# Between the two layers of a diffusion backbone: modulation weights partly into spare expert buffers, a gate store issued by ScalarE, the square-root table fetched early, half of the normalised rows scaled on ScalarE

## The chip, the cores and the metric

One core of a Trainium2 chip runs the whole program. The metric is the device time of one execution in microseconds (us), the median of several runs. The engines are TensorE (PE in the profile; its weight loads are PEld), VectorE (DVE), ScalarE (ACT), GpSimd (POOL) and SyncE (SP, which here only issues transfers). Sixteen DMA engines move the data.

## The reference

Two layers over 1024 latent tokens and 256 context tokens of width 1024, all in 32-bit floats. In each layer:

```python
mod_l = (s_lat @ ada_w[layer] + ada_b[layer])        # six rows: shift, scale, gate, twice
h_l = _rmsnorm(x, norm_mix_g[layer]) * (1.0 + sc_a) + sh_a
p_l = h_l @ w_in[layer]
...
x = x + g_a * (concat(three mixers of p_l, p_c) @ w_out[layer])
h = _rmsnorm(x, norm_ffn_g[layer]) * (1.0 + sc_f) + sh_f
x = x + g_f * _ec_ffn(h, router_w, exp_w1, exp_w3, exp_w2)     # 16 experts
```

The modulation rows depend on the conditioning alone, not on `x`. Layer 1 reads the `x` that the last expert of layer 0 has added to.

## The kernel before

A layer runs in stages: projection, three mixers, output projection, routing, 16 experts. Two places matter here: the start of a projection, in either layer, and the seam where layer 0's experts end and layer 1's projection begins (1880 us to 1920 us of the span).

**Experts** (`moe`). Expert weights arrive by SP's queue in 1 MB tiles `ew`, in a ring of 6 buffers (pool `raws`). ScalarE rounds each to `ewH` and VectorE takes the rest as `ewL`, and TensorE multiplies. Gathered tokens lie in `xg0`, their transpose in `xT0`, its two halves of precision in `xH` and `xL`, all in the pool `wk`, two buffers each, for expert e and e+1. The last product of an expert is added to `x` in memory (the tensor `xd`, and `xc` for the context) by an accumulating scatter that GpSimd issues (L1961).

**Modulation** (`ada_steps`). A third of a layer's modulation, called block b, is a product of a 1024 by 2048 slice of `ada_w` with the conditioning: 8 loads, 32 matmuls per half of them (L159, `adaw`), a bias (L298, tile `mod`), four transposes, a copy (L309, `modT`) and small copies into the tables `modS` and `modA`. Layer 1's blocks 0 and 1 are computed in layer 0's `moe`: block 0 during routing, block 1 after the last expert. With `raws` given, each of its 8 loads is 1 MB into a buffer of the expert ring (L269). Block 1 also holds a gate, which two transfers store to memory (L304).

**Projection** (`project`, `norm_T`). For each 128 tokens: a load `xt` (L362), a sum of squares on ScalarE (L381) for even tiles and on VectorE (L378) for odd ones, for each two tiles a root on ScalarE (L384) and a reciprocal on VectorE (L385), the scaled row `xn` on VectorE (L388), transposes on TensorE (L393), then scale and shift by the modulation on ScalarE (L400, `h`), rounding (L401) and the rest (L402). `first` does the four tiles of block 0 before any product can start; block 1 (four tiles) and the context block (two) are interleaved with the products of the block before. A projection weight arrives as `raw` (L476, two buffers), ScalarE rounds it (L169, `wH`), GpSimd takes the rest (L170, `wL`).

**What sets the order.** A scheduler orders the instructions of each engine when the program is built; routing and the first expert's fetch keep their written order. Each engine, and each engine's queue of transfers, runs its list strictly in that order: a transfer that waits holds all transfers behind it in the same queue.

Of the kernel before, what the change touches and what calls it, by code (L numbers as in the profile page):

```python
# [138 lines left out]
class Net:  # L139
# [115 lines left out]

    def ada_steps(self, l, b, wp, nk, raws=None):

# [4 lines left out]
        w = I["ada_w"][l]  # L262
        st = {}

        def load(i):
            wt = []
            if raws:
                t = raws.tile([128, 4, 512], F32, name="adaw", tag="ew")
                nc.sync.dma_start(t.rearrange("p g c -> p (g c)"), w[i * 128:(i + 1) * 128, 2048 * b:2048 * b + 2048])  # L269
                st["w", i] = [t[:, g:g + 1] for g in range(4)]  # L270
                return
            for g in range(4):
                t = wp.tile([128, nk, 512], F32, name="adaw", tag=f"w{g}")
                c0 = (4 * b + g) * 512
                nc.sync.dma_start(t, w[i * nk * 128:(i + 1) * nk * 128, c0:c0 + 512].rearrange("(k p) c -> p k c", p=128))
                wt.append(t)
            st["w", i] = wt
# [18 lines left out]
        def end():  # L296
            m = wp.tile([128, 512], F32, name="mod", tag="mod", bufs=1)
            nc.vector.tensor_tensor(m, st["ps"], st["bias"], op=OP.add)  # L298
            if b:
                n, g0 = (2, 0) if b == 1 else (5, 2)  # L300
                self.gates[l, n] = self.dr.tile([2, 1024], F32, name=f"gate{l}_{n}")
                for h in range(2):
                    p = 32 * (g0 + h)
                    nc.sync.dma_start(self.gates[l, n][:, h * 512:h * 512 + 512], m[p:p + 2])  # L304
            pt = self.wide()
# [47 lines left out]
    def norm_T(self, wk, hH, hL):  # L353
# [15 lines left out]
        def rows(xts, order=(None, None)):  # L369
# [4 lines left out]
            for i, xt in enumerate(xts):  # L374
# [7 lines left out]
                if i % 2 == 1:  # L382
# [3 lines left out]
                    for j in (i - 1, i):  # L386
                        xn = wk.tile([128, 1024], F32, name="xn", tag="xn", bufs=4)
                        nc.vector.tensor_scalar(xn, xts[j], rs[:, j:j + 1], None, op0=OP.mult)  # L388
                        xns.append(xn)
# [50 lines left out]
    def project(self, es):  # L440
# [10 lines left out]

        nc.scalar.activation(self.sm.tile([128, 1], F32, name="sq0"), self.eps, AF.Sqrt)
        xns = rows(load(0))
# [1324 lines left out]
    def moe(self):  # L1778
# [4 lines left out]
        with ExitStack() as es:  # L1783
# [182 lines left out]
            if wc:  # L1966
                ap = es.enter_context(self.pool("adas", side="right"))
                ada = {b: self.ada_steps(l + 1, b, ap, 1, raws) for b in range(2)}
                ada[0].pop(0)()
# [20 lines left out]
            for e in range(NE):  # L1990
# [16 lines left out]
                st, xT = nxt, xT_next  # L2007
            second(*before)
            for f in ada.get(1, ()):
                f()  # L2010
# [21 lines left out]
```

## Time and profile before

| | us |
|---|---|
| median of 3 runs (lowest to highest) | 3513.27 (3511.27 to 3517.01) |
| the profiled execution | 3507.08 |
| its span in the profile | 3505.3 |
| PE busy | 3257.1 (93%) |
| DVE busy | 2305.1 (66%) |
| ACT busy | 1768.1 (50%) |
| POOL busy | 674.2 (19%) |

The span is the time between the first and the last instruction; the profiled execution took 1.8 us more than that, and 6.2 us less than the median. A busy PE is not PE at its peak, since matmuls are pipelined. The profile's other views list who waited for whom, every instruction in order of time, and each transfer from issue to landing.

### The profile page before, as it was taken

To read this page: it belongs to the slowest core of one execution; us is meant where nothing else is said; L and a number is where in the kernel's file an instruction comes from. 1 tells how busy PE (TensorE), PEld (TensorE's weight loads), DVE (VectorE), ACT (ScalarE), POOL (GpSimd) and SP (SyncE) were. 2 spreads that over 40 slices of the span, in tenths; PEclk is the share of its full clock that TensorE was granted. 3 is DMA by queue.
4 is the path that set the end of the run, shared out by engine and by line. 5 is a ranking of instruction groups with operands and counts; after the bars stand their busy time and mean duration, and the time that the engine had idled before them with its cause. 6 is when DMAs were issued, how large, how long until landed. Compare 5 with 4: busy or idle time off the path is not lost. (4 is left out here: it accounts for less than half of the span.)

```text
span 3505.3 us, 57411 instructions
## 1 busy us (share of the span) xinstructions
PE 3257.1 (93%) x21541; PEld 2444.8 (70%) x21541; DVE 2305.1 (66%) x4661; ACT 1768.1 (50%) x2911; POOL 674.2 (19%) x696
## 2 busy tenths in 40 slices
PE   7998989999996999999997998889999959999996
PEld 4897777766773777777774797778666737777774
DVE  5117748766466888778775315748765468888886
ACT  4116636644422666666663204636545227766674
POOL 2114501034300111111112213500145000000010
PEclk9999989999997999999998999989999979999998
DMA  6633273310336888888888433371401368999997
GB/s 228 194 130 119 95 235 106 114 35 13 114 111 249 287 295 299 289 294 288 296 287 276 150 98 101 106 246 53 129 7 35 138 222 325 388 357 371 352 350 281
DMA packets 266967, 706.50 MB, mean 202 GB/s; under 512 B 25520, under 2 KB 94896, under 8 KB 264640
## 3 DMA queue, kind: packets, MB, share of 16 engines
q1 hardware_dynamic: 239600, 642.94, 51.7%
q0 software_dynamic: 12432, 38.28, 4.7%
q10 hardware_dynamic: 14656, 21.60, 1.8%
q8 instruction: 170, 2.79, 0.3%
q14 instruction: 109, 0.89, 0.1%
HBM read 611.74 MB, written 91.00 MB: 200 GB/s over the span
## 5 line engine op out<-in xcount | busy, mean ns | idle before, releaser
L1817 DVE TENSOR_TENSOR ewL<-ew,ewH 128x1024 fp32r<-128x1024 f32 x705 | 839.7, 1220 | 164.5 <-ACT ewH L1814 153.3
L1814 ACT CAST ewH<-ew 128x1024 fp32r<-128x1024 f32 x705 | 715.9, 1049 | 308.4 <-DMA ew<-in_w 164.6
L159 PE MATMUL pwide<-ewH,xH 128*128 128x512 f32 x930 | 376.8, 405 | 0.0
L159 PE MATMUL pwide<-ewH,xL 128*128 128x512 f32 x930 | 363.6, 391 | 0.0
L159 PE MATMUL pwide<-ewL,xH 128*128 128x512 f32 x930 | 355.3, 394 | 3.6 <-DVE ewL L1817 3.3
L1289 ACT ACTIVATE P<-pwide 128x512 f32<-128x512 f32 (+1 forms) x292 | 151.7, 530 | 179.1 <-PE pwide L159 165.8
L1297 POOL TENSOR_TENSOR sum<-sum,P 128x512 f32<-128x512 f32 (+1 forms) x168 | 189.4, 1151 | 271.0 <-ACT P L1289 267.7
L159 PE MATMUL pwide<-hH,wH 128*128 128x512 f32 (+1 forms) x616 | 234.3, 381 | 0.3 <-ACT wH L169 0.3
L159 PE MATMUL pwide<-hL,wH 128*128 128x512 f32 (+1 forms) x616 | 230.2, 374 | 0.6 <-POOL hL L402 0.5
L159 PE MATMUL pwide<-hH,wL 128*128 128x512 f32 (+1 forms) x616 | 229.9, 373 | 0.7 <-POOL wL L170 0.7
L159 PEld LDWEIGHTS pwide<-ewH,xH 128*128 128x128 f32 x930 | 174.6, 188 | 45.2 <-issue 7.6
L1961 POOL DMA_INDIRECT xd<-y,idx x31 | 65.2, 2102 | 725.1 <-DVE y L1952 705.0
L159 PEld LDWEIGHTS pwide<-ewL,xH 128*128 128x128 f32 x930 | 172.0, 188 | 44.8 <-DVE ewL L1817 8.4
L159 PEld LDWEIGHTS pwide<-ewH,xL 128*128 128x128 f32 x930 | 174.9, 188 | 35.7 <-issue 2.9
L159 PE MATMUL pwide<-ewH,aH 128*128 128x512 f32 x480 | 197.1, 411 | 1.4 <-ACT ewH L1814 1.3
L1829 POOL DMA_INDIRECT xg<-xn,idx x32 | 47.7, 1490 | 759.5 <-PE pwide L159 226.5
L1266 DVE TENSOR_REDUCE mx<-pwide 128x1 f32<-128x512 f32 (+1 forms) x300 | 159.9, 585 | 47.6 <-PE pwide L159 47.4
L159 PE MATMUL pwide<-ewH,aL 128*128 128x512 f32 x480 | 187.7, 391 | 0.8 <-DVE aL L170 0.8
L159 PE MATMUL pwide<-ewL,aH 128*128 128x512 f32 x480 | 183.0, 395 | 0.8 <-DVE ewL L1817 0.8
L159 PE MATMUL pwide<-wH,hH 128*128 128x256 f32 (+3 forms) x480 | 156.6, 326 | 0.0
L159 PE MATMUL pwide<-wL,hH 128*128 128x256 f32 (+3 forms) x480 | 154.0, 321 | 0.0
L159 PE MATMUL pwide<-wH,hL 128*128 128x256 f32 (+3 forms) x480 | 153.7, 320 | 0.0
(391 smaller groups left out, 7100.5 us busy)
## 6 DMA issues: line engine op xcount, KB each, us to landing
ew<-in_w SPq DMA_DIRECT2D x196, 1024.0 KB, 6.4
ew<-in_w SPq DMA_DIRECT2D x329, 512.0 KB, 7.0
adaw<-in_ada_w SPq DMA_DIRECT2D x96, 256.0 KB, 4.0
ewn<-in_w SPq DMA_DIRECT2D x47, 512.0 KB, 5.1
raw<-in_w_in SPq DMA_DIRECT2D x32, 512.0 KB, 7.1
adaw<-in_ada_w SPq DMA_DIRECT2D x16, 1024.0 KB, 9.0
bias<-in_na_bias SPq DMA_DIRECT2D x12, 928.0 KB, 11.9
xt<-in_x SPq DMA_DIRECT2D x16, 512.0 KB, 4.1
```

Source lines behind the costliest of these rows:

```text
L159: self.nc.tensor.matmul(out, a, b, start=start, stop=stop, **kw)
L1266: nc.vector.tensor_reduce(mx[:, j:j + 1], ps[:, :n], op=OP.max, axis=AX.X)
L1289: nc.scalar.activation(P[:, :n], ps[:, :n], AF.Exp)
L1297: eng.tensor_tensor(b.sum[hh][:, :n], b.sum[hh][:, :n], P[:, :n], op=OP.add)
L1814: nc.scalar.copy(H, raw)
L1817: nc.vector.tensor_tensor(Lo, raw, H.bitcast(F32), op=OP.subtract)
L1829: nc.gpsimd.indirect_dma_start(out=g, out_offset=None, in_=quarters(self.xn[1]) if r else self.xn[0], in_offset=bass.IndirectOffsetOnAxis( ...
L1961: nc.gpsimd.indirect_dma_start(out=dst, in_=src, in_offset=None, out_offset=bass.IndirectOffsetOnAxis(ap=ix, axis=0), compute_op=OP.add)
```

## The change

Four edits, none of which changes what is computed. Layer 1's modulation block 1 keeps four of its eight loads in the expert ring; the other four (rows 4 to 7) go, each as two halves of 512 KB, into the two buffers of `xg0`, `xT0`, `xH` and `xL`. The gate of a block computed that way is stored by ScalarE's queue. A root of a constant stands after the last expert, in place of the one at the start of layer 1, so that the table for roots is loaded there. Of the scaled rows `xn` the odd ones are computed by ScalarE, in both layers.

```diff
@@ ada_steps
+        wp_spare, spare = spare or (None, ())
 
         def load(i):
             wt = []
+            if raws and i >= 8 - len(spare):
+                st["w", i] = []
+                for h, tag in enumerate(spare[i - 8]):
+                    t = wp_spare.tile([128, 8, 128] if tag != "xg0" else [128, 1024], F32, name="adaw", tag=tag, bufs=2)
+                    t = t.rearrange("p a b -> p (a b)") if tag != "xg0" else t
+                    c0 = 2048 * b + 1024 * h
+                    nc.sync.dma_start(t, w[i * 128:(i + 1) * 128, c0:c0 + 1024])
+                    st["w", i] += [t[:, None, g * 512:g * 512 + 512] for g in range(2)]
+                return
             if raws:
@@ ada_steps, end
-                    nc.sync.dma_start(self.gates[l, n][:, h * 512:h * 512 + 512], m[p:p + 2])
+                    (nc.scalar if raws else nc.sync).dma_start(self.gates[l, n][:, h * 512:h * 512 + 512], m[p:p + 2])
@@ norm_T, rows
-                        nc.vector.tensor_scalar(xn, xts[j], rs[:, j:j + 1], None, op0=OP.mult)
+                        if j % 2:
+                            nc.scalar.activation(xn, xts[j], AF.Identity, scale=rs[:, j:j + 1])
+                        else:
+                            nc.vector.tensor_scalar(xn, xts[j], rs[:, j:j + 1], None, op0=OP.mult)
@@ project
-        nc.scalar.activation(self.sm.tile([128, 1], F32, name="sq0"), self.eps, AF.Sqrt)
+        if l == 0:
+            nc.scalar.activation(self.sm.tile([128, 1], F32, name="sq0"), self.eps, AF.Sqrt)
@@ moe
-                ada = {b: self.ada_steps(l + 1, b, ap, 1, raws) for b in range(2)}
+                spare = wk, (("xg0", "xg0"), ("xT0", "xT0"), ("xH", "xH"), ("xL", "xL"))
+                ada = {b: self.ada_steps(l + 1, b, ap, 1, raws, spare if b else ()) for b in range(2)}
@@ moe, after second(*before)
+            if not end:
+                self.tc.keep_in_program_order(nc.scalar.activation(self.sm.tile([128, 1], F32, name="sq0"), self.eps, AF.Sqrt))
```

The lists of the built programs differ in two places only: at the start of layer 0's projection, and from the last two experts to the context block of layer 1's projection. In the changed program line numbers are some ten to twenty higher.

SP's queue at the seam, before (`ew` are the experts' weights, `adaw` the modulation's, `raw` the projection's, `xt` token rows):

```order
L1806 DMA ew<-in_w 128x2x1024 x186
L269 DMA adaw<-in_ada_w 128x2048 x4
L476 DMA raw<-in_w_in 128x8x128
L269 DMA adaw<-in_ada_w 128x2048 x4
L476 DMA raw<-in_w_in 128x8x128 x2
L362 DMA xt<-xd_9827 128x1024
L304 DMA gate_2_18855<-mod 2x512 x2
L362 DMA xt<-xd_9827 128x1024 x3
L476 DMA raw<-in_w_in 128x8x128 x2
L362 DMA xt<-xd_9827 128x1024 x4
```

The same stretch of SP's queue with the change:

```order
L1820 DMA ew<-in_w 128x2x1024 x4
L274 DMA adaw<-in_ada_w 128x1024 x2
L1820 DMA ew<-in_w 128x2x1024 x4
L274 DMA adaw<-in_ada_w 128x1024
L1820 DMA ew<-in_w 128x2x1024 x2
L274 DMA adaw<-in_ada_w 128x1024
L1820 DMA ew<-in_w 128x2x1024 x2
L279 DMA adaw<-in_ada_w 128x2048 x4
L490 DMA raw<-in_w_in 128x8x128 x3
L372 DMA xt<-xd_9827 128x1024 x4
L490 DMA raw<-in_w_in 128x8x128
L372 DMA xt<-xd_9827 128x1024 x4
```

The eight half loads stand among the last 22 `ew` loads of 192 (four of them ahead of the first row shown); the four `xt` of block 0 stand together, with no gate store and no `adaw` between the first `raw` and them.

ScalarE's list at the seam, before (L1814 rounds expert weights, L169 a projection weight):

```order
L1814 CAST ewH<-ew 128x1024
L169 CAST wH<-raw 128x1024 x2
L309 COPY modT<-pwide 128x512
L169 CAST wH<-raw 128x1024
L381 ACTIVATE junk,ss_18898<-xt 128x1024
L384 ACT_TABLE_LOAD
L384 ACTIVATE rs_18899<-ss_18898,eps 128x2
L381 ACTIVATE junk,ss_18898<-xt 128x1024
L169 CAST wH<-raw 128x1024
L384 ACTIVATE rs_18899<-ss_18898,eps 128x2
L169 CAST wH<-raw 128x1024
L400 ACTIVATE h_18990<-pone,modS_86,modA_85 128x512
```

The same stretch with the change:

```order
L2026 ACT_TABLE_LOAD
L2026 ACTIVATE sq_18802<-eps 128x1
L169 CAST wH<-raw 128x1024 x3
L314 DMA gate_2_18865<-mod 2x512 x2
L319 COPY modT<-pwide 128x512
L391 ACTIVATE junk,ss_18906<-xt 128x1024
L394 ACTIVATE rs_18907<-ss_18906,eps 128x2
L391 ACTIVATE junk,ss_18906<-xt 128x1024
L399 ACTIVATE xn<-xt,rs_18907 128x1024
L394 ACTIVATE rs_18907<-ss_18906,eps 128x2
L169 CAST wH<-raw 128x1024
L399 ACTIVATE xn<-xt,rs_18907 128x1024
```

The table load stands ahead of the three casts; the gate store stands between the third cast and `modT`; two `xn` have come in, the second behind the cast of the fourth `raw`.

ScalarE's list in layer 0 where the context block is normalised, before (L559 and L539 need the table for exponentials, L384 the one for roots):

```order
L381 ACTIVATE junk,ss_494<-xt 128x1024
L400 ACTIVATE h_481<-pone,modS_81,modA_80 128x512
L400 ACTIVATE h_490<-pone,modS_81,modA_80 128x512
L384 ACTIVATE rs_495<-ss_494,eps 128x2
L169 CAST wH<-raw 128x1024
L559 ACT_TABLE_LOAD
L559 ACTIVATE sC<-pwide 128x512
L539 ACT_TABLE_LOAD
L539 ACTIVATE lb<-lb 128x8
```

And with the change:

```order
L413 ACTIVATE h_481<-pone,modS_81,modA_80 128x512
L394 ACT_TABLE_LOAD
L394 ACTIVATE rs_495<-ss_494,eps 128x2
L413 ACTIVATE h_490<-pone,modS_81,modA_80 128x512
L573 ACT_TABLE_LOAD
L573 ACTIVATE sC<-pwide 128x512
L399 ACTIVATE xn<-xt,rs_495 128x1024
L169 CAST wH<-raw 128x1024
```

The cast of the fifth `raw`, and with it GpSimd's work on that weight, has moved behind the scaled row; ScalarE's list holds six table loads from its start to the end of the context block in both programs.

## Rows read from the trace of the kernel before

**Rows 1.** Busy time of each engine in two stretches of the seam (granted clock, DMA share, GB/s last)

```profile
1880.00:1900.00 20.00, 10.18 (x72) 1.68 (x62) 0.96 (x2) 1.43 (x2) 4.92 (x3) 0.74 1.03 323
1900.00:1917.00 17.00, 4.74 (x24) 3.90 (x25) 10.83 (x13) 8.28 (x12) 9.83 (x4) 0.67 0.82 255
```

**Rows 2.** Waits of PE, 1865 to 1925 us: total, times, longest

```profile
PE pone L393 <- DVE xn L388: 12.0, 3, 8.4
PE pwide L159 <- DMA adaw<-in_ada_w: 9.3, 4, 4.0
```

**Rows 3.** PE in order of time: start, us, operation, count

```profile
1880.09 3.62 PE L159 MATMUL pwide<-adaw,s 128*32 128x512 f32 x32
...
1918.76 0.78 PE L159 MATMUL pwide<-hH,wH 128*128 128x512 f32 x1
```

**Rows 4.** SP's queue in order of time: start, us that issuing took

```profile
1877.09 0.38 SPq L476 DMA_DIRECT2D raw<-in_w_in  x1
1879.51 3.81 SPq L269 DMA_DIRECT2D adaw<-in_ada_w  x4
1885.87 8.32 SPq L476 DMA_DIRECT2D raw<-in_w_in  x1
1894.28 3.52 SPq L362 DMA_DIRECT2D xt<-xd  x1
1900.24 0.57 SPq L304 DMA_DIRECT2D gate<-mod  x2
1900.85 1.29 SPq L362 DMA_DIRECT2D xt<-xd  x3
```

**Rows 5.** Transfers, issue to landing: two of 1870 to 1900 us, L1961, the page

```profile
raw<-in_w_in SPq DMA_DIRECT2D x3, 512.0 KB, 16.2
xd<-y,idx POOLq DMA_INDIRECT x1, 12.8
...
DMA to landing us min/median/max: 7.2/10.4/14.2
...
raw<-in_w_in SPq DMA_DIRECT2D x32, 512.0 KB, 7.1
```

**Rows 6.** ACT in order of time, at the seam

```profile
1900.96 0.59 ACT L309 COPY modT<-pwide 128x512 f32<-128x512 f32 x1 [0.29 <-PE pwide L307]
1901.44 1.05 ACT L169 CAST wH<-raw 128x1024 fp32r<-128x1024 f32 x1
1902.60 1.06 ACT L381 ACTIVATE junk<-xt 128x1024 f32<-128x1024 f32 x1
...
1906.65 1.28 ACT L384 ACT_TABLE_LOAD   x1 [2.90 <-DVE junk L378]
...
1917.16 2.12 ACT L400 ACTIVATE h<-pone,modS,modA 128x512 f32<-128x512 f32 x3 [4.78 <-PE pone L393]
```

**Rows 7.** DVE in order of time, at the seam

```profile
1905.34 1.22 DVE L378 SCALAR_TENSOR_TENSOR junk<-xt 128x1024 f32<-128x1024 f32 x1 [2.14 <-DMA xt<-xd]
...
1908.47 1.42 DVE L388 TENSOR_SCALAR xn<-xt,rs 128x1024 f32<-128x1024 f32 x2
...
1911.65 4.88 DVE L388 TENSOR_SCALAR xn<-xt,rs 128x1024 f32<-128x1024 f32 x2
```

**Rows 8.** POOL in order of time, at the seam

```profile
1879.48 1.55 POOL L1961 DMA_INDIRECT xd<-y,idx  x1 [12.69 <-DVE y L1952]
...
1883.50 2.33 POOL L170 TENSOR_TENSOR wL<-raw,wH 128x1024 fp32r<-128x1024 f32 x1 [0.61 <-ACT wH L169]
```

**Rows 9.** PE in order of time, later blocks: layer 0, then layer 1

```profile
58.45 0.52 PE L393 MATMUL pone<-ident,xn 128*128 128x128 f32 x3 [4.24 <-DVE xn L388]
75.73 0.52 PE L393 MATMUL pone<-ident,xn 128*128 128x128 f32 x3 [2.97 <-DVE xn L388]
...
1946.27 0.52 PE L393 MATMUL pone<-ident,xn 128*128 128x128 f32 x3 [2.05 <-DVE xn L388]
```

**Rows 10.** Busy time of each engine in a stretch of the experts

```profile
1752.00:1840.00 88.00, 88.00 (x686) 63.82 (x682) 68.51 (x86) 54.25 (x66) 10.46 (x6) 1.00 0.82 286
```

More of the change, by code (lines that the diff above doesn't have):

```diff
@@ L254, in ada_begin, with ada_steps @@
             self.ng.append(ng)
-    def ada_steps(self, l, b, wp, nk, raws=None):
+    def ada_steps(self, l, b, wp, nk, raws=None, spare=()):
         nc, I = self.nc, self.I
```

## The prediction

> **What bounds the kernel now.** The page gives TensorE as busy for 93% of the span, so I looked for the stretches where it is not, with the windows view. Experts and projections run at or near full; the seam between the layers does not: from 1880 to 1900 us TensorE is busy for 10.18 of 20 us, and for 4.74 of the next 17 [rows 1]. The waits view says for what: 9.3 us for `adaw`, 12.0 us for scaled rows `xn` [rows 2].
>
> The timelines show how these hang together. The last expert's product ends at 1880.09, and 32 modulation matmuls follow at once in 3.62 us [rows 3]; their four loads had landed. The other four loads go out only at 1879.51 [rows 4], because they need buffers of the expert ring. From there the DMA engines are full (share 1.03 [rows 1]) and SP's queue stands: the third `raw` takes 8.32 us to issue, the first `xt` 3.52 us, until 1897.80, and the other three `xt` stand behind the gate store, which waits for the modulation, until 1900.85 [rows 4]. So the loads that come too late also delay the rows that have nothing to do with them. The second `xt` lands at 1905.34 (VectorE's square starts there), a table load of 1.28 us sits before the root, the last two rows take 4.88 us where the first two took 1.42 [rows 6, 7], and the first `h` comes at 1917.16 [rows 6], the first product at 1918.76 [rows 3].
>
> All of this stretch leads to that `h`, and what comes after it moves as a whole. I therefore price the change by when that `h` can come.
>
> **Term A: the seam.** Step by step, with the lists of the changed program.
>
> 1. *Modulation.* All eight loads are issued before the last product ends. 64 matmuls at 3.62/32 us are 7.24 us [rows 3]: they end at 1887.3, ahead of the rows.
> 2. *SP's queue.* The second `raw` goes right behind the first (1877.5). The third needs that buffer back, which GpSimd's `wL` releases at 1883.50 + 2.33 = 1885.83 [rows 8]; it starts at 1885.87, as before [rows 4], but without 4 MB ahead of it.
> 3. *The scatter.* The `xt` read what the last scatter wrote. It is issued at 1879.48 [rows 8] and took 12.8 us beside the full DMA; scatters take 10.4 in the median and 7.2 at the least [rows 5]. So it lands between 1886.7 and 1892.3. I take 9.5 us, between least and median because less is under way: 1889.0.
> 4. *The rows' loads.* The second `xt` took 1905.34 - 1900.85 = 4.5 us [rows 4, 7], and the four issue in about 1.7. It lands at 1893.9.
> 5. *ScalarE's list.* Third `raw`: 7.1 us (the page's median [rows 5]) after 1885.87, 1893.0. Its cast 1.05, two gate issues 0.57 as on SP, `modT` 0.59 [rows 4, 6]: 1895.2. From the start of the squares to the first row is 1908.47 - 1905.34 = 3.13 us, less the table load 1.85 [rows 6, 7], so the first pair can begin at 1897.1. ScalarE has then a square, a row, a root, a cast and a row: four at 1.05 and an estimated half for the root and the sums, from 1896.8 to about 1901.6. The last rows no longer wait on VectorE. From the end of the rows to `h` is 1917.16 - 1916.53 = 0.63 us [rows 6, 7]: **1902.2, or 15.0 us earlier**. I take 14.5, since VectorE's square can overlap a `wL` on GpSimd.
>
> Ends: with all loads early, ScalarE's list still holds (1893.0 by the third `raw`), so -16. If the third `raw` takes 16.2 us as it did here at worst [rows 5], step 5 starts 9.1 us later: -6.
>
> The table load is worth 1.28 us by its row, and it is in step 5; the early load falls where ScalarE is idle. By contrast "ScalarE: Activation LUTs", section What ACT_TABLE_LOAD costs, of the Trainium skill counts a drain of about 1.38 us beside the load, 2.66 in all. By that the sum would be 1.4 us better; the trace, where the root starts right as the 1.28 us end, does not show the drain.
>
> The gate store: after step 1 the modulation is there before the scatter lands, so on SP it would cost no wait any more, only 0.57 us; on ScalarE it costs the same and is counted. I give it nothing more.
>
> TensorE's clock: the granted share is 0.74 and 0.67 in the two stretches [rows 1], so part of it ran at the 1.2 GHz level after TensorE stood. It will stand again, from 1888 to about 1898, so I count no gain.
>
> **Term B: half of the rows on ScalarE, later blocks.** Ten of twenty `xn` move: a ScalarE pass over 128x1024 takes 1.05, VectorE's 0.71 alone and 2.4 when it is held up [rows 6, 7]. In layer 0, TensorE waits 4.24 us for block 1's first row and 2.97 for the context's [rows 9]. The first wait stays: that row stays on VectorE behind the same squares. The second should nearly go, because the fifth weight's cast and its GpSimd work now stand behind the row; about 3, and 0.5 more at the second pair. In layer 1 the context's wait is 2.05 [rows 9]; I take 1.5. ScalarE's extra passes lie beside TensorE's products. Sum 5, ends 0 and 9 (all the waits of rows 9).
>
> For block 0 of layer 0, which waits for its own modulation, I count nothing.
>
> **Term C: the experts.** 4 MB more move under the last two experts, where the DMA share is 0.82 and TensorE is busy for 88 of 88 us [rows 10]. 18% of 88 us is 16 us of free DMA time; 4.2 MB at 0.323 MB/us [rows 1] are 13. It fits; ends 0 and +2.
>
> **Sum.** -14.5 - 5 = -19.5 against the profiled execution's 3507.08 us: 3487.6. The median of the runs is 6.2 us above that execution; on it, **3494**.
>
> **Rivals.**
>
> *The third `raw` stays slow* (16.2 us). For: the projection's weights come in 512-byte pieces and share the engines with the scatter. Against: 4 MB less beside them. Term A is then 6, B as before: -11, 3502. Chance 0.12.
>
> *The moved loads are paid in the experts.* The bytes are not fewer; if the `ew` loads come later by their whole DMA time, 13 us, TensorE stands there, and -19.5 becomes -6.5, 3507. For: each spare half stands ahead of `ew` tiles in one queue. Against: TensorE shows no wait in that stretch, and the free DMA time is larger than the need [rows 10]. Chance 0.08. This is what "DMA: Bandwidth & Descriptors", Rules for kernel authors, of the Trainium skill points to: all queues run on the same 16 engines, and spreading transfers saves only issue time.
>
> *SP's queue still stands* (slower). The fourth `raw` goes behind four `xt`, and ScalarE's cast of it stands ahead of the last row. If each `xt` takes 8.32 us to issue, as the third `raw` did [rows 4], it goes out at 1889.0 + 33.3 = 1922.3, lands 7.1 later, and with 1.05 + 1.05 + 0.63 `h` comes at 1932.1: 15 later, less term B +10, 3523. It ends slower once an `xt` takes some 6 us. Against: three `xt` took 1.29 together once the loads were through. Chance 0.04.
>
> *The change doesn't do what it says*: a spare load waits for the last expert's buffer and holds the `ew` behind it, so nothing is gained. Against: in the list, the two that wait for the last expert's `xH` and `xL` stand ahead of `ew` tiles whose ring buffers the same product holds, so nothing behind them could go sooner. Within 0.2%, 3513. Chance 0.04.
>
> **How the numbers follow.** The forecast has 0.72. About 0.2% (7 us) is what a measurement can tell from no change. Faster by more: 0.72, two thirds of the first rival and a third of the second, 0.83. Within: the rest of these and the last, 0.13. Slower: 0.04. The range takes the ends, -6 to -25, and the spread of the runs: 3485 to 3508.
>
> **What would show it.** In the changed profile: no TensorE wait for `adaw` after the last product; modulation matmuls ending near 1887; four `xt` issued together near 1889; no table load between square and root; first `h` near 1902; `xn` 1.05 us on ScalarE; the context's wait in layer 0 under 1 us. Wrong would be: waits for `ewL` or `ewH` in the last two experts, an `xt` that takes several us to issue, or ScalarE standing at a `raw` until after 1900.

## The result, and the profile after

| | us, median (lowest to highest, runs) | against the kernel before beside it | ratio, 95% interval |
|---|---|---|---|
| changed kernel | 3496.34 (3486.41 to 3506.46, 6) | 3515.64 (6) | 0.9945 [0.9932, 0.9957] |
| the same, run again | 3496.01 (3490.94 to 3505.28, 6) | 3518.04 (16) | 0.9941 [0.9920, 0.9962] |

The change makes the kernel some 19 to 22 us faster. The forecast was 3494 in a range of 3485 to 3508.

One thing must be known before the traces are read. The execution that was profiled is the longest of its six, 3506.46 us, 0.6 us below the profiled execution of before. Aligned instruction by instruction on ScalarE, the two traces differ so (my own working; time in the trace before, and how much later the same instruction starts in the trace after):

```
   186.9  -1.5     after the start of layer 0
  1852.5  +9.6     experts of layer 0, unchanged code
  1940.2  -8.9     after the seam
  2455.2  -8.6
  2788.7  -1.1
  3460.6  -1.6     near the end
```

The gains stand where the change is: 1.5 us at the start of layer 0, some 16 at the seam (the last expert's product ends 7.2 us later than before, so from +7.2 to -8.9), as the timelines below show in whole. Elsewhere, in code that is the same in both, this execution lost some 16 us again on balance, and I put that down to the stretches in which TensorE was granted half its clock (its mean granted clock is 0.961, against 0.963 in the trace before and 0.964 in the rerun's). The rerun's trace kept what it had gained at the seam (its instructions stand 10 to 13 us earlier from there to the end). So I read the seam relative to the end of the last expert's product, which is the first modulation matmul behind it: 1880.09 before [rows 3], 1887.29 after.

The windows view, for the 20 and the next 17 us from that point (columns as in rows 1: length, busy time of PE, PEld, DVE, ACT and POOL with counts, granted clock, DMA share, GB/s):

```profile
1887.00:1907.00 20.00, 11.39 (x96) 5.90 (x85) 6.27 (x12) 9.43 (x13) 10.83 (x6) 0.83 0.93 262
1907.00:1924.00 17.00, 13.67 (x69) 10.36 (x67) 14.81 (x22) 13.00 (x19) 10.67 (x5) 1.00 0.60 170
```

Against [rows 1], the second stretch went from 4.74 busy us of TensorE to 13.67, and its granted clock from 0.67 to 1.00. The waits view of TensorE, 1860 to 1930 us (total, times, longest):

```profile
PE pone L406 <- DVE xn L401: 8.0, 2, 7.8
PE pwide L159 <- POOL hL L415: 2.0, 2, 1.3
```

The 9.3 us for `adaw` of [rows 2] are gone, and the 12.0 for `xn` are 8.0. The 2.0 us for `hL` stand behind the first `h`. TensorE in order of time, to be read against [rows 3]:

```profile
1887.29 7.05 PE L159 MATMUL pwide<-adaw,s 128*32 128x512 f32 x64
...
1908.84 0.50 PE L159 MATMUL pwide<-hH,wH 128*128 128x512 f32 x1
```

All 64 modulation matmuls run in one go, and the first projection product comes 21.6 us after the last expert's product; before it was 38.7. SP's queue, against [rows 4]:

```profile
1884.28 9.17 SPq L490 DMA_DIRECT2D raw<-in_w_in  x3
...
1893.09 0.37 SPq L490 DMA_DIRECT2D raw<-in_w_in  x1
...
1893.55 2.26 SPq L372 DMA_DIRECT2D xt<-xd  x4
```

The group of three `raw` spans 9.17 us because its third waits for a buffer; by its own row (the second shown, from a narrower window) that third one is issued at 1893.09 in 0.37 us, where it took 8.32 before, and four `xt` take 2.26 together. The transfers of that time, issue to landing:

```profile
raw<-in_w_in SPq DMA_DIRECT2D x3, 512.0 KB, 6.4
xt<-xd SPq DMA_DIRECT2D x3, 512.0 KB, 6.2
xd<-y,idx POOLq DMA_INDIRECT x1, 6.7
```

The scatter into `xd` landed in 6.7 us instead of 12.8 [rows 5]. ScalarE, VectorE and GpSimd at the seam, against [rows 6 to 8]:

```profile
1874.85 1.28 ACT L2026 ACT_TABLE_LOAD   x1
...
1897.52 1.04 ACT L169 CAST wH<-raw 128x1024 fp32r<-128x1024 f32 x1 [5.35 <-DMA raw<-in_w_in]
1897.60 0.76 ACTq L314 DMA_DIRECT2D gate<-mod  x2
1898.68 0.58 ACT L319 COPY modT<-pwide 128x512 f32<-128x512 f32 x1
...
1903.41 1.14 ACT L399 ACTIVATE xn<-xt,rs 128x1024 f32<-128x1024 f32 x1
...
1905.83 1.15 ACT L399 ACTIVATE xn<-xt,rs 128x1024 f32<-128x1024 f32 x1
1907.55 2.12 ACT L413 ACTIVATE h<-pone,modS,modA 128x512 f32<-128x512 f32 x3 [0.57 <-PE pone L406]
```

```profile
1900.12 1.95 DVE L388 SCALAR_TENSOR_TENSOR junk<-xt 128x1024 f32<-128x1024 f32 x1 [5.02 <-DMA xt<-xd]
...
1902.70 0.75 DVE L401 TENSOR_SCALAR xn<-xt,rs 128x1024 f32<-128x1024 f32 x1
...
1898.64 2.35 POOL L170 TENSOR_TENSOR wL<-raw,wH 128x1024 fp32r<-128x1024 f32 x1 [3.26 <-ACT wH L169]
```

The first `h` starts 20.3 us after the last product (1907.55), 37.1 before (1917.16 [rows 6]). The rows of the later blocks, against [rows 9], and a stretch of the experts, against [rows 10]:

```profile
58.81 0.45 PE L406 MATMUL pone<-ident,xn 128*128 128x128 f32 x1 [4.26 <-DVE lbm L551]
...
76.07 0.52 PE L406 MATMUL pone<-ident,xn 128*128 128x128 f32 x3 [1.31 <-DVE xn L401]
82.48 0.44 PE L406 MATMUL pone<-ident,xn 128*128 128x128 f32 x2 [1.66 <-ACT h L413]
...
1937.39 1.24 PE L406 MATMUL pone<-ident,xn 128*128 128x128 f32 x6 [2.06 <-DVE xn L401]
```

```profile
1752.00:1840.00 88.00, 88.00 (x683) 63.63 (x671) 69.64 (x87) 54.63 (x65) 10.66 (x6) 1.00 0.88 321
```

TensorE is busy for 88 of 88 us in this stretch although the DMA share rose from 0.82 to 0.88: here the moved loads cost nothing. Behind it they cost a little. The last two spare loads go out at 1853 and 1855 us, ScalarE then waits for an expert weight, and TensorE waits for `aL`, the rest behind the rounded input of the last expert's second product. First the trace before, then the trace after:

```profile
1865.61 0.50 PE L159 MATMUL pwide<-ewH,aL 128*128 128x512 f32 x1 [0.24 <-DVE aL L170]
```

```profile
1862.10 2.00 ACT L1828 CAST ewH<-ew 128x1024 fp32r<-128x1024 f32 x2 [4.55 <-DMA ew<-in_w]
...
1872.79 0.50 PE L159 MATMUL pwide<-ewH,aL 128*128 128x512 f32 x1 [0.64 <-DVE aL L170]
```

ScalarE waited at most 1.75 us for an `ew` there before. In the nine traces of kernels with the spare loads the last product comes 0.4 to 1.8 us later by this wait (0.4 here, 1.8 in the rerun), in the four of changed kernels without them 0.0 to 0.2. That cost lies ahead of the point from which I count the seam, so it has to be taken off what the seam gains.

### The profile page after: what moved, and what is told of

Same layout as the page of the kernel before. It is cut to its first block, busy times and chain, and to the rows that moved or that the text cites. A ratio compares the mean times of both kernels' runs of the same rounds, so it can differ in the third digit from the quotient of the medians.

```text
span 3504.7 us, 57419 instructions
## 1 busy us (share of the span) xinstructions
PE 3262.5 (93%) x21541; PEld 2453.8 (70%) x21541; DVE 2297.0 (66%) x4651; ACT 1778.1 (51%) x2921; POOL 674.0 (19%) x696
## 5 line engine op out<-in xcount | busy, mean ns | idle before, releaser
L159 PE MATMUL pwide<-ew,xT 128*32 128x256 f32 (+1 forms) x2112 | 154.5, 390 | 0.0
```

The source lines that it names most:

```text
L159: self.nc.tensor.matmul(out, a, b, start=start, stop=stop, **kw)
```

## The experiments

Three landmarks serve for all of them, taken from each run's trace, since single executions of one kernel differ by 10 to 20 us: the first `h` after the last expert's product; the 151st projection product after it (the expectations call it the 150th), which also holds what follows the first `h`; and the shift against the trace of before at 187 us, which is what layer 0's start gained or lost. (The expectations' "22.8 us" for the first projection product is the end of the second; the first came at 21.6.)

| kernel | first h | 151st product | layer 0 | median us | ratio to before, 95% interval |
|---|---|---|---|---|---|
| before | 37.1 | 86.7 | 0 | | |
| whole change | 20.3 | 70.4 | -1.5 | 3496.34 | 0.9945 [0.9932, 0.9957] |
| whole change, again | 21.2 | 71.4 | -1.9 | 3496.01 | 0.9941 [0.9920, 0.9962] |
| spare buffers alone | 22.5 | 74.3 | +0.3 | 3512.16 | 0.9982 [0.9969, 0.9996] |
| gate store alone | 35.0 | 83.1 | +1.8 | 3517.17 | 1.0004 [0.9990, 1.0017] |
| rows alone | 37.1 | 86.5 | -0.8 | 3512.99 | 0.9988 [0.9973, 1.0002] |
| table load alone | 33.1 | 84.9 | +0.9 | 3515.91 | 1.0003 [0.9992, 1.0014] |
| without spare buffers | 29.7 | 79.9 | -1.5 | 3510.12 | 0.9979 [0.9965, 0.9993] |
| without gate store | 20.7 | 72.3 | -2.2 | 3503.39 | 0.9969 [0.9958, 0.9980] |
| without rows | 21.8 | 73.2 | -0.5 | 3507.63 | 0.9980 [0.9963, 0.9998] |
| without table load | 22.2 | 72.6 | -0.9 | 3502.90 | 0.9972 [0.9957, 0.9987] |
| whole, third raw buffer | 22.1 | 70.0 | -0.8 | 3503.81 | 0.9959 [0.9943, 0.9974] |
| whole, rows exchanged | 21.6 | 69.8 | -6.0 | 3498.94 | 0.9949 [0.9930, 0.9967] |
| whole, both | 22.5 | 70.2 | -4.7 | 3494.25 | 0.9929 [0.9905, 0.9954] |

The two traces of the whole change differ by 1.0 us in the seam's landmarks and by 0.4 in layer 0's, but layer 0's spread more over kernels that have the same code there: -0.5 to +1.8 in the five with all rows on VectorE (before is one of them), -0.8 to -2.2 in the six with the whole change's rows and two `raw` buffers. The means are +0.5 and -1.5, so the rows are worth some 2 us there. Differences near these sizes are read with care below.

### The spare buffers alone

```diff
-                    (nc.scalar if raws else nc.sync).dma_start(self.gates[l, n][:, h * 512:h * 512 + 512], m[p:p + 2])
+                    nc.sync.dma_start(self.gates[l, n][:, h * 512:h * 512 + 512], m[p:p + 2])
```

(from the changed kernel, with the rows and the table load also put back)

> Only the modulation weights of block 1 go partly into spare buffers; gate stores on SP, all rows on VectorE and the table load between square and root stay as before. Measure at the seam: from the first modulation matmul after the last expert's product to the first projection product, 38.7 us before, 22.8 us after. Theory L (the four late loads fill the DMA engines and hold SP's queue, so they delay the rows): most of the gain is here, the seam takes 24 to 27 us, no transfer of SP takes over 3 us to issue, and the time is 11 to 15 us below before. Theory G (the rows stood behind the gate store in SP's queue, the loads were only beside it): the seam keeps over 32 us, the gain is under 6 us. Theory S (ScalarE's and VectorE's order of squares, rows and table load sets the seam's end): the seam keeps over 30 us, since this order is as before.

The first product comes 23.8 us after the last expert's, and nothing on SP takes long. SP's queue in this kernel:

```profile
1897.73 1.48 SPq L372 DMA_DIRECT2D xt<-xd  x3
1899.30 0.56 SPq L314 DMA_DIRECT2D gate<-mod  x2
1899.91 0.35 SPq L372 DMA_DIRECT2D xt<-xd  x1
```

So theory L holds for the seam: this part alone takes the first `h` from 37.1 to 22.5 us, against 20.3 with everything. Three of the four `xt` now go ahead of the gate store. In the time theory L missed: it fell by 0.18%, some 6 us [1 to 11], where 11 to 15 were expected, and less than the 12.4 us by which the 151st product came sooner (11.6 less what the spare loads cost ahead of the seam); more on that below.

### The whole change without the spare buffers

```diff
-                ada = {b: self.ada_steps(l + 1, b, ap, 1, raws, spare if b else ()) for b in range(2)}
+                ada = {b: self.ada_steps(l + 1, b, ap, 1, raws, ()) for b in range(2)}
```

> The whole change without the spare buffers: the four late loads go out after the last product again. Theory L: the third raw piece takes some 8 us to issue again, the seam takes 33 to 37 us, and the gain over before is 2 to 6 us (gate store off SP's queue, table load, rows in layer 0). Theory G: the rows are free of the gate store, the seam takes 23 to 28 us and 10 us or more of the gain stay. Theory S: the seam takes under 30 us, 8 us or more stay.

The late loads bring the slow issue back: of the 9.41 us of the two `raw` in SP's queue, 2.9 are a wait for GpSimd's `wL` by the waits view, and the other 6 or so are issue:

```profile
1889.05 9.41 SPq L490 DMA_DIRECT2D raw<-in_w_in  x2
1898.55 3.53 SPq L372 DMA_DIRECT2D xt<-xd  x1
```

Here the first product comes at 31.0 us, between what theories L (33 to 37) and G or S (under 30) wanted, and some 7 us of the gain remain. So the four late loads are the largest part, 9.5 us at the 151st product, but the three small parts together give 6.8 there without them, more than theory L allowed.

### The gate store alone

```diff
-                    nc.sync.dma_start(self.gates[l, n][:, h * 512:h * 512 + 512], m[p:p + 2])
+                    (nc.scalar if raws else nc.sync).dma_start(self.gates[l, n][:, h * 512:h * 512 + 512], m[p:p + 2])
```

> Only the two gate stores of each block are issued by ScalarE. Theory L: the last three row loads no longer stand from 1897.80 to 1900.85 for the store, so the seam is at most 3 us shorter (35.5 to 38.7 us), the time 0 to 3 us less. Theory G: the seam falls by 8 us or more. Theory S: no change at the seam within 1 us.

The first `h` comes 2.0 us sooner, the 151st product 3.6; theory G falls. Standing behind the store cost what [rows 4] show, 1897.80 to 1900.85, and no more.

### The rows alone

The edit is the change's own one in `rows`.

> Only every second normalised row goes to ScalarE (block 0 of layer 0 included). By the forecast: layer 0 gains some 3 us (the context's wait in layer 0 falls from 2.97 us to under 1), layer 1's blocks some 1.5, and at the seam the last two rows come some 2 us sooner (they took 4.88 us on VectorE, the first two 1.42): 3 to 7 us in all. Rival (the rows only trade VectorE's delay for ScalarE's list, as the casts stand there): layer 0 gains 1 to 2 us, nothing in layer 1, 0 to 2 us at the seam: 1 to 4 us in all, which 3 rounds would hardly tell from no change, so the landmarks of the trace decide.

At the seam nothing: 37.1 and 37.1, where the forecast wanted 2 us. VectorE's and GpSimd's timelines of this kernel show why:

```profile
1914.60 2.55 DVE L401 TENSOR_SCALAR xn<-xt,rs 128x1024 f32<-128x1024 f32 x1
...
1914.25 2.35 POOL L170 TENSOR_TENSOR wL<-raw,wH 128x1024 fp32r<-128x1024 f32 x1 [5.85 <-ACT wH L169]
```

GpSimd's `wL` began 0.35 us before VectorE's third row, and that row ended 0.55 us after `wL` did; undisturbed it takes 0.75. Half of the rows had left VectorE, but the third is still one of its own and stands in the same place. The rule that fits is in the Trainium skill, "SBUF — State Buffer", section SBUF: two separate sides: VectorE, in some of its instructions, and GpSimd share a pair of ports, which whoever starts first keeps for its whole instruction. By that rule the row would end at 1916.60 + 0.75 = 1917.35 at the latest; the trace has 1917.15. In layer 0 the shift is -0.8, against +0.6 in the mean of the four kernels whose rows are all on VectorE: the rival's 1 to 2 us, and not the forecast's 3.

### The table load alone

```diff
+        if l == 0:
+            nc.scalar.activation(self.sm.tile([128, 1], F32, name="sq0"), self.eps, AF.Sqrt)
...
+            if not end:
+                self.tc.keep_in_program_order(nc.scalar.activation(self.sm.tile([128, 1], F32, name="sq0"), self.eps, AF.Sqrt))
```

> Only the load of the root's table is fetched ahead, under the end of the experts. Measure at the seam from the first modulation matmul after the last expert's product: 38.7 us to the first projection product in the kernel before. By the load's own row (1.28 us, and the root starts as it ends): first product 37.2 to 37.6 us, i.e. 1.1 to 1.5 us sooner. By the Trainium skill's price (ScalarE: Activation LUTs, What ACT_TABLE_LOAD costs: the load and a drain of ScalarE before it, an estimate of 2.7 us): 36.0 us. Rival (the last rows and squares on VectorE set the end, ScalarE's load lies beside them): under 0.5 us. In the time of the whole kernel none of these shows in 3 rounds; the trace's landmarks decide.

The first `h` comes 4.0 us sooner, more than any of the three expected. The rows of this kernel:

```profile
1908.84 0.30 ACT L394 ACTIVATE rs<-ss,eps 128x2 f32<-128x2 f32 x1 [2.81 <-DVE junk L388]
...
1912.55 1.42 DVE L398 TENSOR_SCALAR xn<-xt,rs 128x1024 f32<-128x1024 f32 x2
...
1913.33 2.85 POOL L170 TENSOR_TENSOR wL<-raw,wH 128x1024 fp32r<-128x1024 f32 x1 [5.67 <-ACT wH L169]
```

VectorE's sum ended at 1908.74 and the root began 0.10 us later; before, it began 1.37 us later with the load between [rows 6, 7]. So the load itself is worth 1.27 us, its row and no more. But those 1.3 us put the last two rows ahead of GpSimd's `wL`, and they took 1.42 us where they took 4.88 [rows 7]: a second saving of 3.5 us, of which the `h` kept 2.7. At the 151st product 1.8 of the 4.0 are left, and the time shows none of it (1.0003).

### The whole change without the table load

```diff
-        if l == 0:
-            nc.scalar.activation(self.sm.tile([128, 1], F32, name="sq0"), self.eps, AF.Sqrt)
+        nc.scalar.activation(self.sm.tile([128, 1], F32, name="sq0"), self.eps, AF.Sqrt)
...
-                self.tc.keep_in_program_order(nc.scalar.activation(self.sm.tile([128, 1], F32, name="sq0"), self.eps, AF.Sqrt))
```

> The whole change with the table load back between squares and root. In the whole change the first h comes 20.3 us after the last expert's product and the 150th projection product 70.4 us after. If ScalarE's list sets the end, as forecast: h at 21.5 to 21.7 us (the 1.28 us of the row); by the Trainium skill's price with the drain some 23 us; if VectorE or TensorE set the end, under 20.8.

The first `h` comes at 22.2 us, 1.9 and 0.9 later than in the two traces of the whole change, 1.4 in the mean. ScalarE in this kernel:

```profile
1900.61 1.28 ACT L394 ACT_TABLE_LOAD   x1 [2.05 <-DVE junk L388]
1901.90 0.29 ACT L394 ACTIVATE rs<-ss,eps 128x2 f32<-128x2 f32 x1
```

Again the root starts as the 1.28 us end, 1.37 us after VectorE's sum. The forecast's price stands for the root; the `h` lies above the 21.5 to 21.7 expected, and ScalarE's list sets it here: its last two rows stand together, and two casts end just before the `h` starts (1907.58).

### The whole change without the gate store

```diff
-                    (nc.scalar if raws else nc.sync).dma_start(self.gates[l, n][:, h * 512:h * 512 + 512], m[p:p + 2])
+                    nc.sync.dma_start(self.gates[l, n][:, h * 512:h * 512 + 512], m[p:p + 2])
```

> The whole change with the two gate stores of each block back on SP. Forecast: with the modulation done 7 us after the last product and the row loads going out behind it, the store costs its issue alone, 0.57 us, or nothing: h at 20.3 to 21.0 us after the last product (whole change 20.3). Rival (the store holds SP's queue until the modulation is copied, some 8 us after the last product, and the row loads behind it wait): h at 22 us or later.

The first `h` comes at 20.7 us, between the two traces of the whole change: once the modulation is early, it does not matter for the rows which queue stores the gate. The 151st product is 0.9 and 1.9 us later; from the first product to it the granted clock is 0.93 in this trace and 0.97 in both traces of the whole change.

### The whole change without the rows

```diff
-                        if j % 2:
-                            nc.scalar.activation(xn, xts[j], AF.Identity, scale=rs[:, j:j + 1])
-                        else:
-                            nc.vector.tensor_scalar(xn, xts[j], rs[:, j:j + 1], None, op0=OP.mult)
+                        nc.vector.tensor_scalar(xn, xts[j], rs[:, j:j + 1], None, op0=OP.mult)
```

> The whole change with all normalised rows on VectorE. With the late loads gone, the squares come about 11.9 us after the last expert's product. Theory (the four rows in turn on VectorE, held up beside GpSimd, are the seam's last piece once loads, table and store are gone): h at 22 to 24 us after the last product instead of 20.3, the 150th projection product 2 to 4 us later than 70.4; and layer 0 loses its 1.5 us. Rival (rows alone gave nothing at the seam of the kernel before, 37.06 against 37.07 us, so they give nothing here): h within 0.5 us of 20.3.

The first `h` is at 21.8 us (0.5 and 1.5 later), the 151st product 1.8 and 2.8 later, layer 0 loses 1.0 and 1.4. The reason for the seam was not the expected one. VectorE and GpSimd in this kernel:

```profile
1900.22 1.42 DVE L398 TENSOR_SCALAR xn<-xt,rs 128x1024 f32<-128x1024 f32 x2
...
1903.40 1.42 DVE L398 TENSOR_SCALAR xn<-xt,rs 128x1024 f32<-128x1024 f32 x2
...
1904.30 2.73 POOL L170 TENSOR_TENSOR wL<-raw,wH 128x1024 fp32r<-128x1024 f32 x1 [5.79 <-ACT wH L169]
```

Both pairs run undisturbed; here GpSimd is the one that starts later. What ScalarE's rows save is only that two rows are made side by side.

### Is the size right: the whole change again

No edit.

> The whole change once more, with more executions. Its first six gave 19.3 us less than before, of which the landmarks of the trace show 1.5 in layer 0 and 16.3 at the seam (150th projection product 70.4 us after the last expert's product, 86.7 before). Theory A (the forecast's sum is right to a few us): 15 to 20 us less again. Theory B (the first six were favoured by where TensorE's half clock fell, as executions of one kernel differ by 10 to 20 us through it): 11 to 15 us less, as the four kernels less one part (7 to 12 less) and the single parts (5 + 7 for the two halves) point to. In the trace either way: h 20 to 20.7 us after the last product.

0.9941 [0.9920, 0.9962], some 21 us less [13 to 28]. That is just above theory A's 15 to 20 and far from theory B: the first six were not favoured. The `h` came at 21.2 us, later than expected; the scatter took 8.1 us in this trace, 6.7 in the first.

### A third buffer for the projection's raw weights

```diff
-        wr = es.enter_context(self.pool("wraw", bufs=2, side="right"))
+        wr = es.enter_context(self.pool("wraw", bufs=3, side="right"))
```

> The whole change with a third buffer for the projection's raw pieces, so that SP's third raw need not wait for GpSimd (in the whole change it is issued 5.8 us after the last expert's product and the four xt right behind it). Theory P (the third raw is the last thing ahead of the rows, in SP's queue, on the DMA engines and with its wL beside VectorE's square): the square on VectorE starts 1 to 3 us sooner than 12.8 us after the last product, and h comes 17.5 to 19.5 us after it instead of 20.3. Theory Q (the rows wait for the scatter, which lands 6.1 us after the last product, so the third raw only filled that time): xt goes out no sooner, h within 0.7 us of 20.3. In the time 0 to 3 us less than the whole change, at the edge of what 5 rounds tell.

The reason is theory Q's, but the `h` at 22.1 us lies outside the windows of both. The scatter took 9.1 us beside the earlier `raw` transfers (6.7 and 8.1 in the two traces of the whole change), and the rows wait for it. Transfers and SP's queue of this kernel:

```profile
xd<-y,idx POOLq DMA_INDIRECT x1, 9.1
```

```profile
1889.10 1.76 SPq L372 DMA_DIRECT2D xt<-xd  x4
```

The `xt` go out 8.5 us after the last product (1880.63 here), 6.3 in the changed kernel. VectorE's square ran without GpSimd beside it (1.27 us instead of 1.95), which gave only part of that back. The 151st product is not later for it (70.0 against 70.4 and 71.4), and the time, 0.9959 [0.9943, 0.9974], is no better than the whole change's.

### The rows exchanged, and both together

```diff
-                        if j % 2:
+                        if j % 2 == 0:
```

> The whole change with the first and third row of each block on ScalarE and the second and fourth on VectorE, the other way round. In layer 0 of the whole change TensorE still waits 4.3 us at 58.8 us for block 1's first row, which VectorE makes in 2.58 us (56.09 to 58.67) while ScalarE's row takes 1.15 (56.03 to 57.18). By the forecast's reason (the wait stays because that row stays on VectorE): the wait falls by 1.5 us at least and layer 0 ends 1 to 1.5 us sooner. Rival (the transposes need three rows in turn, and VectorE's becomes the second): the first wait falls, but the time is waited at the next transposes, and layer 0 ends within 0.5 us of before. At the seam h 0.3 to 0.6 us later (ScalarE's row takes 1.15 us there, VectorE's 0.75).

TensorE in layer 0 of this kernel:

```profile
57.20 0.33 PE L406 MATMUL pone<-ident,xn 128*128 128x128 f32 x1 [1.55 <-ACT xn L399]
58.83 0.77 PE L406 MATMUL pone<-ident,xn 128*128 128x128 f32 x5 [1.30 <-DVE xn L401]
```

The wait of 4.26 us becomes 1.55 and 1.30: part of it is waited again at the second row, as the rival said, but 1.4 us are saved. VectorE and GpSimd in the changed kernel show what it was:

```profile
56.09 2.58 DVE L401 TENSOR_SCALAR xn<-xt,rs 128x1024 f32<-128x1024 f32 x1
```

```profile
51.45 6.67 POOL L170 TENSOR_TENSOR wL<-raw,wH 128x1024 fp32r<-128x1024 f32 x2
```

The first row ends at 58.67, 0.55 us behind GpSimd's `wL`, as the third row at the seam did. (The view names `lbm` as the releaser of that wait, a short sum that VectorE does right behind the row.) On ScalarE the row is ready without it. The context's two waits of the changed kernel, 1.31 and 1.66, become one of 0.9, and one of 0.3 for `h` is new in block 1. Together that is 3.2 us, and layer 0 ends 6.0 us earlier than before instead of 1.5, which is 4.5. The rest goes with the clock. The windows from 57 to 64 us, first of the changed kernel, then of this one:

```profile
57.00:64.00 7.00, 5.19 (x17) 4.29 (x18) 3.48 (x10) 3.49 (x6) 1.11 (x1) 0.52 0.94 294
```

```profile
57.00:64.00 7.00, 5.47 (x28) 4.18 (x28) 3.38 (x10) 5.05 (x9) 1.09 (x1) 1.00 0.83 269
```

Behind the wait of 4.26 us TensorE ran at a granted 0.52, its level of 1.2 GHz but for a little; behind the two short ones at 1.00, and did 28 matmuls instead of 17. The kernel with both edits has the same short waits and yet a granted 0.76 there, so a short wait does not exclude it. At the seam the first `h` came 0.4 and 1.4 us later than in the two traces of the whole change, against 0.3 to 0.6 expected. So layer 0's remaining wait was VectorE's row, as the forecast had said. In the time nothing can be told from the whole change: 0.9949 [0.9930, 0.9967].

> Both together, the third raw buffer and the rows the other way round. If the two are independent: the seam of the kernel with the third buffer plus 0.3 to 0.6 us, and layer 0 as in the kernel with the rows exchanged; in the time between 15 and 22 us less than before if the whole change itself gives 15 to 20.

Fastest by its median, 3494.25 of four executions, some 24 us less than before, but its interval lies over that of the whole change: no better version is shown.

## Why the prediction was right

**The sum.** Forecast -19.5, measured 19 to 22 by the two medians. By landmarks the changed places gave 1.5 to 1.9 in layer 0 and 15.3 to 16.3 at the seam, less the 0.4 and 1.8 us ahead of it: 17.3 in the first trace and 15.4 in the rerun. So the seam is about as forecast, the rows of the later blocks gave less, and the other 2 and 7 us of the two medians are shown at no place that the change touches: that the median came so near to 3494 is in part luck. That the changed kernel's profiled execution, 3506.46, stands far from the 3487.6 of the forecast is, as I read the traces, the half clock in unchanged stages, which the forecast's bridge by 6.2 us from execution to median could not know.

**Term A, seam.** Forecast: first `h` 15.0 us earlier, counted as 14.5; by the two traces 16.8 and 15.8. By its steps, after the last product:

| step | forecast | measured |
|---|---|---|
| modulation ends | 7.2 | 7.05 |
| third `raw` issued | 5.8 | 5.8 |
| scatter issue to landing | 9.5 | 6.7 (8.1 in the rerun) |
| second `xt` there (square on VectorE) | 13.8 | 12.8 |
| first pair of rows can begin | 17.0 | 15.4 |
| first `h` | 22.1 | 20.3 (21.2) |

Each step is there, and three transfers were sized wrongly, in both directions. I took the scatter between its least and its median, but with no late loads beside it, it took 6.7 to 8.1 us in seven traces, about its least of before, 7.2 [rows 5]. The third `raw` was taken at 7.1 us, and its cast began 4.4 us after its issue (1893.09 to 1897.52). Against that, the `xt` took 6.2 us in the median where I had 4.5. Two details fell otherwise: the gate stores took 0.76 us on ScalarE's queue, not 0.57, and ScalarE's list did not set the end of the first pair. VectorE's square did, held up beside `wL` (1.95 us, alone 1.22), the overlap for which I had kept half a us.

**The mechanism** (late loads hold the DMA engines and SP's queue) is shown from both sides: alone, moving them gives 14.6 of the 16.8 us at the first `h`, and without that the third `raw` takes some 6 us to issue again and 9.5 us of the gain are lost. No run frees the queue without the scatter. By the rows the queue was the later of the two before (third `raw` issued by 1894.19, scatter landed at 1892.3 [rows 4, 5]); with the change they tie, 6.2 and 6.1 us after the last product, and in the rerun the scatter is last, at 7.5.

One assumption of the sum held only roughly: what comes after the first `h` does not quite move as a whole. Of the 16.8 and 15.8 us 16.3 and 15.3 are left at the 151st product, and of the spare buffers' 14.6 alone 12.4.

**Table load.** 1.28 us forecast, 1.27 measured between sum and root, in the old order and the new. The rule that the prediction set against it, in the Trainium skill's "ScalarE: Activation LUTs", What ACT_TABLE_LOAD costs, of a drain beside the load, is not seen at this place: the 4.0 us that the load alone gave come from the collision that it moved, not from a drain. ScalarE had stood idle before that load. Where it works up to the load, in layer 0 of the changed kernel, there is no drain to see either:

```profile
71.75 0.78 ACT L413 ACTIVATE h<-pone,modS,modA 128x512 f32<-128x512 f32 x1 [1.26 <-POOL hL L415]
72.54 1.28 ACT L394 ACT_TABLE_LOAD   x1
73.84 0.30 ACT L394 ACTIVATE rs<-ss,eps 128x2 f32<-128x2 f32 x1
```

**Gate store.** Forecast as worth nothing beyond its issue once the loads are early: right (20.7 against 20.3 and 21.2). On the kernel before it is worth 2.0 us at the first `h` and 3.6 at the 151st product, and nothing that shows in the time (1.0004).

**Term B.** Half right. The first wait of layer 0 stayed (4.26), and the context's fell, but to 1.31 and not under 1, and a new wait for `h` of 1.66 came behind it: the two are 2.97 us again, as much as before [rows 9]. Layer 0 gave 1.5 to 1.9 us instead of 3.5. What its waits lost is two short ones of the trace before, behind the rows of [rows 9], 0.9 us together:

```profile
62.77 0.55 PE L393 MATMUL pone<-ident,xn 128*128 128x128 f32 x3 [0.61 <-DVE xn L388]
...
77.33 0.90 PE L393 MATMUL pone<-ident,xn 128*128 128x128 f32 x3 [0.28 <-DVE xn L388]
```

The rest, 0.6 to 1.0 us, is not traced to a wait; some of it may be clock, which was 0.50 from 76.2 to 79.6 us before and 1.00 in both traces of the whole change, while it was also low for longer around 60 us in the first of them. Layer 1's context kept its wait, 2.06 against 2.05 [rows 9], where I had taken 1.5 off: that row is VectorE's own and is still held up (1.74 us). The step that failed is "the second should nearly go, because the fifth weight's cast and its GpSimd work now stand behind the row"; it went by 1.7 us, and as much came back as a wait for ScalarE's `h`. Term A's surplus made up for part of it.

**Term C.** Nearly nothing, within the ends of 0 and +2: TensorE waits for no `ewL` or `ewH`, but 0.4 and 1.8 us longer for the last expert's `aL` and `aH`, a wait that the forecast did not name.

**TensorE's clock.** I counted no gain. From the first product to the 151st it took 48.0 us before and 48.9 after, but the two are made up differently. The windows of this stretch, first of the trace before, then of the trace after:

```profile
1918.76:1966.78 48.02, 44.73 (x205) 35.57 (x203) 31.89 (x60) 25.07 (x41) 13.97 (x9) 0.92 0.45 147
```

```profile
1908.84:1957.70 48.86, 43.55 (x205) 34.16 (x204) 32.19 (x57) 29.54 (x46) 16.75 (x10) 0.97 0.52 168
```

For the same products TensorE was busy 1.2 us less at a granted 0.97 instead of 0.92, and stood 2.0 us longer; its waits for GpSimd's `hL` rose from 0.3 to 2.0 us. So there was a gain by the clock, and longer waits took it back.

**Rivals.** The `raw` of the seam took 6.4 us in the median, not 16.2; the moved loads were paid with 0.4 to 1.8 us, not 13; no `xt` took long to issue; the change did what it says.

**What stays open.** At the seam the parts nearly add up (12.4 + 3.6 + 0.1 + 1.8 = 17.9 against 15.3 to 16.3), but in the medians they do not: each kernel that lacks one small part gains 8 to 12 us less than the 19.3 of the whole, and only 1 to 3 of that stands at the seam. The mean granted clock of the executions follows that: 0.959 for before, 0.964 for the whole change in both series, 0.961 to 0.963 without one of the three small parts. So the rest seems to lie in unchanged stages at the half clock; this was not followed stage by stage. Why these should get more of it when a small part is missing, no run here shows.

## What to carry to other kernels

When transfers can't start for lack of a buffer, look at what they meet when they are let go: here four late loads cost far more through the queue and the scatter behind them than through the matmuls that waited for them, and buffers that had just fallen free took them for 0.4 to 1.8 us. Price a small step by what it moves as well as by its own row: 1.28 us of table load alone brought the first `h` 4.0 us forward, because VectorE's rows then missed GpSimd's instruction (1.8 were left at the 151st product), and moving half of the rows was worth nothing in the same place, because the one that remained did not. Where executions of one kernel differ by 10 to 20 us, read a change of this size at landmarks of the trace, relative to the last event that it does not touch, and look whether it does touch that event: here the moved loads pushed the point from which the seam was counted.

## What the runs showed of the hardware that was not expected

- The last scatter's time to landing goes with what else is under way: 10.7 to 13.7 us in the five kernels with 4 MB of late loads beside it, 8.8 and 9.1 in the two with a third `raw` buffer, 6.7 to 8.1 in the seven traces with neither.
- The issue of one transfer on SP took 8.32 us [rows 4] right behind four 1 MB loads, and some 6 in the whole change without the spare buffers; in the whole change, without such loads ahead, 0.37.
- VectorE's scaling of a 128x1024 row takes 0.75 us, or 2.55 and 2.58 where GpSimd's `wL` had begun before it; both then ended 0.55 us after `wL` did.
- A table load took 1.28 us, and where the next instruction waited for nothing else it followed at once, whether ScalarE had been idle or busy before the load.
- Over 79 executions of the kernel before, 3507 to 3530 us, time and mean granted clock (0.955 to 0.963) go together. The two traces of the whole change do not have all stretches at half clock in the same places: from 76 to 80 us neither has one and before has, from 657 to 661 us only the first has one, from 823 to 826 us only the rerun.
